# Output projection of a two-layer decoder trunk: order of its products, of its weight loads and of the block sums

## The chip, the cores and the metric

One core of a Trainium2 chip runs the whole program. The metric is the device time of one execution in microseconds (us), lower is better; the time before is the median of three executions, and the profile is of one further execution.

## The reference, cut to what matters

```python
for l in range(DEPTH):                      # DEPTH = 2, x is (1, 1024, 1024)
    h = rmsnorm(x, norm1[l])
    proj = h @ w_in[l]
    ...                                     # two attention branches o_a, o_b and two gates
    merged = g_a * (o_a @ w_br[l, :OUT_A]) + g_b * (o_b @ w_br[l, OUT_A:])
    x = x + merged @ w_o[l]                 # the output projection: the change is here
    h2 = rmsnorm(x, norm2[l])               # "norm" below
    up = h2 @ w_up[l]
    ...                                     # gated ConvFFN, down projection
return rmsnorm(x, norm_f)
```

## The kernel before, in words

Everything is kept transposed: a chunk of 128 features lies on the 128 partitions, and 512 tokens (half `n`, 0 or 1) lie along a row. A fp32 number is split in two parts, `hi` (a cast by ScalarE, line 129) and `lo` (a subtraction by VectorE, line 130), and one product of a 128-wide block is three matmuls: hi by hi, lo by hi, hi by lo (lines 891 to 893). Half of a contraction of 1024 takes four such blocks, so 12 matmuls; that is called **a product** here.

Ahead of the projection, a loop over 16 chunks (`todo`) multiplies the branch results with the gates (line 1451, tile `gin`), adds them to `mrg` (line 1456), and writes the merged chunk as `hh` (ScalarE, line 1415) and `hl` (GpSimd, line 1416). These are todo 0 to 15; the last four are chunk 6 and 7 of half 0 and chunk 6 and 7 of half 1. The four buffers `p4` that hold `gin` are used again by the tiles `wo_c` of `w_o`: the load of the first `wo_c` starts when todo 12 has been added, the second after todo 13, the third after 14, the fourth after 15.

The projection has 8 output chunks. Chunks 6 and 7 are done plainly, two products for each half (`chunk(n, e)`). Chunks 0 to 5 go in pairs (0,1), (2,3), (4,5) by a seven-product scheme (`p1` to `p7` for a pair). Its weights are sums of four blocks of a pair, made in place by GpSimd (`weight_sums`, lines 1146 to 1149), and its inputs are sums of blocks of the merged input: first `m_sum` (made earlier), second (lines 1265 and 1266, VectorE, in place), third `h_sum` (lines 1271 to 1273, GpSimd), fourth (lines 1278 and 1279, VectorE, in place). Each is split into `t_hi` and `t_lo` (the lists `S[1]` to `S[4]`) when it is made.

`items` lists the products in TensorE's order, and it is the list that sets the order around the change. Product `i` of the list is numbered from 0. Before:

0, 1 `chunk(0,6)`; 2, 3 `chunk(0,7)`; 4, 5 `chunk(1,6)`; 6 `p1(0)`; 7 `p3(0)`; 8 `p1(1)`; 9 `p3(1)`; 10 `p2(0)`; 11 `p2(1)`; 12 `p5(0)`; 13 `p6(0)`; 14 `p5(1)`; 15 `p6(1)`; 16 `p1(2)`; 17 `p7(0)`; 18 `p3(2)`; 19 `p7(1)`; 20 `p6(2)`; 21 `p5(2)`; 22 `p7(2)`; then, beside the norm of half 0, 23 `p2(2)`; 24 to 26 `p4`; 27, 28 `chunk(1,7)`.

Before product `i` is issued, `run` fetches raw weights up to product `i + 4`, splits weights up to product `i + 2` (`prepare`; for a `p1` the weights' sums of its pair follow at once), and makes the block sums that `merged_sums` plans for `i`. TensorE runs in exactly this order; the other engines' streams are set by a scheduler from the order of the code, and each engine then runs its stream in order.

When half 0 of `x` is complete, `norm(0)` sums its squares over features with small matmuls by `ones` (`nrm_t`, line 467), takes the root (ScalarE) and the reciprocal (VectorE, line 470), spreads the result with another group (`nrm_b`, line 476) and scales `x`. The squares are added up chunk by chunk in `norm_add` (line 420), on VectorE where `e % 3` is 1 and on GpSimd otherwise. `drive` interleaves it with products 23 to 28; `norm(1)` follows, interleaved with the first products of the ConvFFN (`u_ps`).

Of the kernel before, what the change touches and what calls it, by code (L numbers as in the profile page):

```python
# [6 lines left out]
F32 = mybir.dt.float32  # L7
# [8 lines left out]
P = 128  # L16
# [36 lines left out]
def trunk_kernel(ctx, tc, x, norm1, w_in, b_gate, w_br, w_o, norm2, w_up, conv_w, conv_b, w_down, norm_f, out, depth=None, probe=None):  # L53
# [355 lines left out]
    def norm_add(n, e, first=False, sub=slice(0, HF), adds=None):  # L409

        if first:
            if n == 0 or ACC[0] is None:
                both = sb.tile([P, 2, HF], F32, tag="ql", bufs=2, name="nrm")
                ACC[0], ACC[1] = both[:, 0, :], both[:, 1, :]
        acc = ACC[n]
        acc = acc[:, sub]
        sq = acc if first else small("sq")[:, sub]
        act.activation(sq, xc(n, e, sub), AF.Square)  # L418
        if not first:
            (adds or (dve if e % 3 == 1 else pool)).tensor_tensor(acc, acc, sq, ALU.add)  # L420
# [704 lines left out]
    def output_products(l, sums):  # L1125
# [4 lines left out]
        def columns(c):  # L1130
            return w_o[l][:, c * P : (c + 1) * P].rearrange("(k p) n -> p k n", p=P)

        def load_pairs():
            for p in range(3):
                if p < 2:
                    t = [sb.tile([P, 2, HF], F32, tag="p4", bufs=4, name="wo_c") for _ in range(2)]
                else:
                    both = sb.tile([P, 4, HF], F32, tag="ql", bufs=2, name="wo_p")
                    t = [both[:, 0:2, :], both[:, 2:4, :]]
                for c in range(2):  # L1140
                    nc.sync.dma_start(t[c].rearrange("p a (k n) -> p (a k) n", n=P), columns(2 * p + c))
                tiles[p] = [t[c][:, k, :] for c in range(2) for k in range(2)]

        def weight_sums(p):
            a11, a12, a21, a22 = tiles[p]
# [5 lines left out]
        def add(n, e, o, full=False):  # L1151
            dve.tensor_tensor(xc(n, e), xc(n, e), o, ALU.add)
            if full:
                norm_add(n, e, e == 6)

        def free(name):
            return lambda key: bank("ps", name)
# [13 lines left out]
        def chunk(n, e):  # L1171
            for k in range(2):
                items.append(
                    (("raw", e, k), (lambda key: plain.setdefault(key, bank("ps", "o_ps"))) , (n, e), lambda n=n, k=k: half(n, k), k == 0, k == 1,
                     (lambda o, n=n, e=e: add(n, e, o, True)) if k else None)
                )
# [36 lines left out]
        chunk(1, 7)  # L1213

        loaded, ready = {}, {}

# [17 lines left out]
                at[name] += 1  # L1234

        def start():
            load_pairs()
            until("fetch", fetch, 2)
            until("prepare", prepare, 2)

# [10 lines left out]
                    done(o)  # L1251
                yield

        return start, lambda: run(0, count), lambda: run(count, len(items))

    def merged_sums(keep):

        def split_into(t, i, r):
            if t not in S:
                new_s(t)  # L1260
            split(*S[t][i], r)

        def second(i):
            r, (h, lo) = keep[i], half(0, 1)[i]
            dve.tensor_tensor(r, f32(h), r, ALU.subtract)
            dve.tensor_tensor(r, r, f32(lo), ALU.add)
            split_into(2, i, r)

        def third(i):
            r, (ah, al), (bh, bl) = small("h_sum"), half(0, 1)[i], half(0, 0)[i]  # L1270
            pool.tensor_tensor(r, f32(al), f32(bl), ALU.subtract)
            pool.tensor_tensor(r, r, f32(ah), ALU.add)
            pool.tensor_tensor(r, r, f32(bh), ALU.subtract)
# [36 lines left out]
    def mixer(l, pending):  # L1310
# [71 lines left out]
        def gate_in(i):  # L1382
            if i < len(todo):
                n, e = todo[i]
                gt = gts[i] = sb.tile([P, 2, HF], F32, tag="p4", bufs=4, name="gin")
                nc.sync.dma_start(gt, gs[e, n])
                for ab in range(2):
                    act.activation(gt[:, ab, :], gt[:, ab, :], AF.Sigmoid, bias=bg[:, 0, ab * KD + e : ab * KD + e + 1])
# [9 lines left out]
                wbs.append(parts_)  # L1398

        kept, sums = {}, {}  # L1400

        def merged(n, e, m):
            if e < 4:
# [28 lines left out]
        for i, ab in order:  # L1432
            n, e = todo[i]
            sl = slice(n * HF, (n + 1) * HF)
            if i not in seen:
                if e == 0:
                    new_h(n)
                if i % 4 == 0:
                    wb = wbs.pop(0)
                if l and i in X_AT:  # L1440
                    x_in(X_AT.index(i) // 2, X_AT.index(i) % 2)
            gt = gts[i]
            ec = slice((e % 2) * P, (e % 2 + 1) * P)
            if "ab"[ab] not in oh:
                in_two("a")
            o = bank("st"[ab], "br_ps")
            (wh, wl), (xh, xl) = wb[ab], oh["ab"[ab]]
            for _ in product(o, [((wh[:, c, ec], wl[:, c, ec]), (xh[:, c, sl], xl[:, c, sl])) for c in range(2)]):
                pass
            with tc.high_priority(offset=AHEAD):  # L1450
                dve.tensor_tensor(gt[:, ab, :], gt[:, ab, :], o, ALU.mult)
# [4 lines left out]
            dve.tensor_tensor(m, gt[:, 0, :], gt[:, 1, :], ALU.add)  # L1456
# [598 lines left out]
```

## Time and profile before

| | before |
|---|---|
| median of three executions | 2776.66 us (2774.24 to 2783.27) |
| profiled execution, whole | 2783.72 us |
| its span, first to last instruction | 2781.9 us |
| TensorE busy | 2675.2 us, 96% |
| VectorE busy | 2182.6 us, 78% |
| ScalarE busy | 1343.6 us, 48% |
| GpSimd busy | 829.5 us, 30% |
| mean granted TensorE clock | 0.983 |

Times are from the start of the span. The projection of layer 0 begins at 632.1 us, that of layer 1 at 2005.9 us. A busy share is an average over stages with different limits, so it says little of a stage of 85 us; the stage is read from what TensorE waits for in it.

### The profile page before, as it was taken

Reading aid. Unit: us, or ns where it says so; the run is one execution under the profiler, and the core shown is the slowest. Engines: PE = TensorE matmul, PEld = TensorE weight load, DVE = VectorE, ACT = ScalarE, POOL = GpSimd, SP = SyncE. Lnnn points to the kernel's source line nnn. Section 1 sums busy time; section 2 is a strip of 40 time slices with the busy share of each in tenths; the row PEclk is TensorE's granted clock in tenths of the full one; section 3 lists DMA queues with packets and bytes.
Section 4 is the critical chain, followed back from the end, with each engine's and each line's share of the span. In section 5 each row is a group of like instructions: output and inputs, shape, how many; then the busy total and the mean of one; then the engine's idle time right before and its main releaser. Section 6 shows DMA issues by size and latency. Waiting matters only on the chain. (4 is left out here: it accounts for less than half of the span.)

```text
span 2781.9 us, 36907 instructions
## 1 busy us (share of the span) xinstructions
PE 2675.2 (96%) x13026; PEld 2232.8 (80%) x13026; DVE 2182.6 (78%) x3186; ACT 1343.6 (48%) x2484; POOL 829.5 (30%) x593
## 2 busy tenths in 40 slices
PE   8999999998899999999999999999988999999999
PEld 7877888886678888888888778888766788888888
DVE  5878866787689888897657887766977888988965
ACT  5666544463455555432345665434634555554225
POOL 2004133236224443321220042332451334443210
PEclk9999999999999999999999999999989999999999
DMA  4023499762134444688401235988602344346863
GB/s 149 27 84 111 130 244 233 206 238 68 53 111 147 152 152 144 217 324 317 151 33 46 80 118 152 254 211 232 223 19 57 121 160 166 137 154 239 322 260 122
DMA packets 391109, 442.56 MB, mean 159 GB/s; under 512 B 21276, under 2 KB 312460, under 8 KB 389388
## 3 DMA queue, kind: packets, MB, share of 16 engines
q1 hardware_dynamic: 390924, 440.20, 49.6%
q8 instruction: 103, 1.69, 0.3%
q14 instruction: 82, 0.67, 0.1%
HBM read 297.46 MB, written 142.67 MB: 158 GB/s over the span
## 5 line engine op out<-in xcount | busy, mean ns | idle before, releaser
L130 DVE TENSOR_TENSOR w_lo<-up_a,w_hi 128x512 fp32r<-128x512 f32 x240 | 237.0, 994 | 22.0 <-ACT w_hi L129 22.0
L129 ACT CAST w_hi<-up_a 128x512 fp32r<-128x512 f32 x240 | 149.3, 622 | 186.3 <-PE u_a L892 45.8
L1811 DVE TENSOR_TENSOR x<-x,d_ps 128x512 f32<-128x512 f32 (+1 forms) x228 | 152.6, 673 | 77.6 <-PE d_ps L1805 76.6
L1542 POOL TENSOR_TENSOR cv<-cv 128x512 f32<-128x512 f32 x88 | 131.8, 1509 | 248.6 <-DVE cv L1537 138.6
L129 ACT CAST w_hi<-in_a 128x512 fp32r<-128x512 f32 x140 | 86.8, 620 | 149.2 <-PE i_a L892 86.8
L130 DVE TENSOR_TENSOR g<-cv,g 128x512 fp32r<-128x512 f32 x154 | 152.3, 990 | 5.3 <-ACT g L129 2.8
L1803 PE MATMUL d_ps<-gd_in,w_hi 128*128 128x512 f32 (+1 forms) x340 | 130.2, 383 | 1.4 <-ACT w_hi L129 1.1
L1805 PE MATMUL d_ps<-gd_in,w_lo 128*128 128x512 f32 (+1 forms) x340 | 129.8, 382 | 0.0
L1804 PE MATMUL d_ps<-gd_in,w_hi 128*128 128x512 f32 (+1 forms) x340 | 129.7, 382 | 0.0
L130 DVE TENSOR_TENSOR w_lo<-w_raw,w_hi 128x512 fp32r<-128x512 f32 x140 | 105.5, 759 | 30.9 <-ACT w_hi L129 30.5
L891 PE MATMUL u_a<-hh,w_hi 128*128 128x512 f32 x320 | 124.7, 390 | 2.2 <-DVE u L1693 2.1
L891 PE MATMUL u_a<-t_hi,w_hi 128*128 128x512 f32 x320 | 124.6, 389 | 0.0
L892 PE MATMUL u_a<-t_lo,w_hi 128*128 128x512 f32 x320 | 124.5, 389 | 0.0
L893 PE MATMUL u_a<-hh,w_lo 128*128 128x512 f32 x320 | 124.5, 389 | 0.0
L892 PE MATMUL u_a<-hl,w_hi 128*128 128x512 f32 x320 | 124.5, 389 | 0.0
L893 PE MATMUL u_a<-t_hi,w_lo 128*128 128x512 f32 x320 | 124.5, 389 | 0.0
L1020 POOL TENSOR_TENSOR in_a<-in_a 128x512 f32<-128x512 f32 x28 | 38.0, 1357 | 277.5 <-DVE w_lo L130 277.5
L130 DVE TENSOR_TENSOR w_lo<-in_a,w_hi 128x512 fp32r<-128x512 f32 x140 | 114.3, 816 | 4.9 <-ACT w_hi L129 4.6
L420 POOL TENSOR_TENSOR nrm<-nrm,sq 128x512 f32<-128x512 f32 x29 | 40.8, 1406 | 255.8 <-ACT sq L418 255.1
L129 ACT CAST w_hi<-w_raw 128x512 fp32r<-128x512 f32 x140 | 86.4, 620 | 60.7 <-PE r_ps L156 15.8
L629 DVE TENSOR_TENSOR_SCAN stay<-stay,zero 128x128 f32<-128x128 f32 (+3 forms) x64 | 89.0, 1390 | 32.2 <-ACT stay L627 31.6
L1803 PE MATMUL d_ps<-gd_in,wd 128*128 128x512 f32 (+1 forms) x292 | 113.9, 390 | 0.0
(438 smaller groups left out, 9057.6 us busy)
## 6 DMA issues: line engine op xcount, KB each, us to landing
gd<-g SPq DMA_DIRECT2D x154, 512.0 KB, 3.5
gd_in<-gd SPq DMA_DIRECT2D x154, 512.0 KB, 6.3
up_a<-in_w_up_dram SPq DMA_DIRECT2D x80, 512.0 KB, 4.7
in_a<-in_w_in_dram SPq DMA_DIRECT2D x56, 512.0 KB, 5.7
w_raw<-in_w_in_dram SPq DMA_DIRECT2D x104, 256.0 KB, 2.9
t_kq<-tk SPq DMA_DIRECT2D x64, 384.0 KB, 8.5
wd_raw<-in_w_down_dram SPq DMA_DIRECT2D x22, 1024.0 KB, 11.9
gin<-gs SPq DMA_DIRECT2D x32, 512.0 KB, 4.0
```

The costliest lines, as they stand in the source:

```text
L129: act.copy(hi, src)
L130: dve.tensor_tensor(lo, src, f32(hi), ALU.subtract)
L420: (adds or (dve if e % 3 == 1 else pool)).tensor_tensor(acc, acc, sq, ALU.add)
L629: dve.tensor_tensor_scan(rev, rev, zero[:, 0:1].to_broadcast([P, L]), 1.0, ALU.mult, ALU.add)
L891: pe.matmul(o, w[0][:, c], rh, start=(first and i == 0), stop=False, skip_group_check=True)
L892: pe.matmul(o, w[0][:, c], rl, start=False, stop=False, skip_group_check=True)
L893: pe.matmul(o, w[1][:, c], rh, start=False, stop=(last and i == 3), skip_group_check=True)
L1542: return lambda: pool.tensor_tensor(dst, a, b, ALU.subtract)
L1803: pe.matmul(o[:, sub], wh[:, c], gh[:, sub], start=(i == 0 and k in (0, 4, 5)), stop=False, skip_group_check=True)
L1804: pe.matmul(o[:, sub], wh[:, c], gl[:, sub], start=False, stop=False, skip_group_check=True)
L1805: pe.matmul(o[:, sub], wl[:, c], gh[:, sub], start=False, stop=(i == m - 1), skip_group_check=True)
L1811: dve.tensor_tensor(x, x, o[:, sub], ALU.add)
```

## The change

In `items`, `p1(0)` and `p1(1)` move from places 6 and 8 to places 2 and 3, and `chunk(1,7)` moves ahead of the three `p4`. The list is then: 0, 1 `chunk(0,6)`; 2 `p1(0)`; 3 `p1(1)`; 4, 5 `chunk(0,7)`; 6, 7 `chunk(1,6)`; 8, 9 `p3(0)`, `p3(1)`; 10 to 23 as before; 24, 25 `chunk(1,7)`; 26 to 28 `p4`. The loads of the pairs' weights are issued one by one inside the loop over todo (from todo 12), and the first fetches and splits (`start`) are called there too. The plan of `merged_sums` is renumbered and calls `split_into(2, ...)` on its own. `drive` runs four steps of the products ahead of `norm(0)`. The square of half 0's chunk 5 is added by VectorE.

```diff
-        def load_pairs():
-            for p in range(3):
...
+        def load(i):
+            p, c = i // 2, i % 2
+            if p < 2:
+                t = sb.tile([P, 2, HF], F32, tag="p4", bufs=4, name="wo_c")
...
+            nc.sync.dma_start(t.rearrange("p a (k n) -> p (a k) n", n=P), columns(i))
...
             if full:
-                norm_add(n, e, e == 6)
+                norm_add(n, e, e == 6, adds=dve if (n, e) == (0, 5) else None)
...
         chunk(0, 6)
+        p1(0)
+        p1(1)
         chunk(0, 7)
         chunk(1, 6)
-        for f, p in ((p1, 0), (p3, 0), (p1, 1), (p3, 1), (p2, 0), (p2, 1)):
+        for f, p in ((p3, 0), (p3, 1), (p2, 0), (p2, 1)):
             f(p)
...
-        for f, p in ((p2, 2), (p4, 0), (p4, 1), (p4, 2)):
-            f(p)
+        p2(2)
         chunk(1, 7)
+        for p in range(3):
+            p4(p)
...
+    def merged_sums(keep):
...
+        def second(i):
+            r, (h, lo) = keep[i], half(0, 1)[i]
+            pool.tensor_tensor(r, f32(h), r, ALU.subtract)
+            pool.tensor_tensor(r, r, f32(lo), ALU.add)
...
     def merged_sums(keep):
...
         for i in range(4):
-            task(i // 2, lambda i=i: split_into(1, i, keep[i]))
-            task(2 + i, second, i)
-            task(6 + 2 * i, third, i)
-            task(8 + 2 * i, lambda i=i: split_into(3, i, third_r[i]))
+            task(1 + i // 2, lambda i=i: split_into(1, i, keep[i]))
+            task(4 + i, second, i)
+            task(8 + i, lambda i=i: split_into(2, i, keep[i]))
+            task(9 + i, third, i)
+            task(12 + i, lambda i=i: split_into(3, i, third_r[i]))
             task(16 + i, fourth, i)
-            task(22, lambda i=i: split_into(4, i, keep[i]))
+            task(24 + i // 2, lambda i=i: split_into(4, i, keep[i]))
...
             gate_in(i + 3)
+            if i == 12:
+                start()
+            if i >= 12:
+                load(i - 12)
...
-        start, early, rest = output_products(l, merged_sums(sums))
-        start()
+        load(4)
+        load(5)
         for _ in early():
             pass
...
-        drive(first_half(), rest(), 0.7)
+        drive(first_half(), rest(), 0.7, 4)
```

The file also defines the functions from `zeros` to `output_products` twice, with the same text, and `merged_sums` twice, with different text. In Python the later definition is the one that is called. The first `merged_sums`, the one with `second` on `pool`, is the earlier; the later one is the old function with the new plan, and in it `second` still reads:

```python
        def second(i):
            r, (h, lo) = keep[i], half(0, 1)[i]
            dve.tensor_tensor(r, f32(h), r, ALU.subtract)
            dve.tensor_tensor(r, r, f32(lo), ALU.add)
            split_into(2, i, r)
```

Lines after the change are about 330 larger for this reason (line 1451 is 1779, 1456 is 1784, 1415 is 1743, 1152 is 1476).

Three places of the new order, all in layer 1. First VectorE at the end of the loop over todo, before; `gin_18279` is todo 14 and `gin_18303` is todo 15, and `t_lo_18405` is a split of a first sum:

```order
L1451 TENSOR_TENSOR gin_18279<-gin_18279,br_ps_18327 128x512
L1451 TENSOR_TENSOR gin_18279<-gin_18279,br_ps_18335 128x512
L1456 TENSOR_TENSOR mrg_18343<-gin_18279 128x512
L1451 TENSOR_TENSOR gin_18303<-gin_18303,br_ps_18347 128x512
L130 TENSOR_TENSOR t_lo_18405<-m_sum_18058,t_hi_18404 128x512 x2
L1451 TENSOR_TENSOR gin_18303<-gin_18303,br_ps_18355 128x512
L130 TENSOR_TENSOR t_lo_18405<-m_sum_18168,t_hi_18404 128x512
L1456 TENSOR_TENSOR mrg_18363<-gin_18303 128x512
```

VectorE at the same place after; `gin_18287` is todo 14, `gin_18311` is todo 15, and `wo_c_18327` is the first loaded tile, with the weights of `p1(0)`:

```order
L1779 TENSOR_TENSOR gin_18287<-gin_18287,br_ps_18351 128x512
L130 TENSOR_TENSOR w_lo_18405<-wo_c_18327,w_hi_18404 128x512
L1779 TENSOR_TENSOR gin_18287<-gin_18287,br_ps_18359 128x512
L130 TENSOR_TENSOR t_lo_18436<-m_sum_18066,t_hi_18435 128x512
L1779 TENSOR_TENSOR gin_18311<-gin_18311,br_ps_18373 128x512
L1784 TENSOR_TENSOR mrg_18367<-gin_18287 128x512
L1779 TENSOR_TENSOR gin_18311<-gin_18311,br_ps_18381 128x512
L130 TENSOR_TENSOR t_lo_18436<-m_sum_18066,t_hi_18435 128x512
L1784 TENSOR_TENSOR mrg_18389<-gin_18311 128x512
```

The split of `p1(0)`'s weights now stands between the two gate products of todo 14, and a split of a first sum has come ahead of `mrg` of todo 14.

Second, ScalarE about products 6 to 9 before; `t_hi_18597` is the third sum's split, and the weights of `p3(0)`, `p1(1)` and `p3(1)` are `w_hi_18522`, `w_hi_18547` and `w_hi_18575`:

```order
L129 CAST w_hi_18522<-wo_c_18371 128x512
L418 ACTIVATE sq_18494<-x0_18091 128x512
L129 CAST w_hi_18547<-wo_c_18375 128x512
L129 CAST t_hi_18597<-h_sum_18555 128x512
L129 CAST t_hi_18455<-m_sum_18194 128x512
L129 CAST t_hi_18597<-h_sum_18601 128x512
L129 CAST w_hi_18575<-wo_c_18375 128x512
```

ScalarE there after; `t_hi_18699` is the third sum's split, `t_hi_18507` is the second sum's, and the weights of `p3(0)`, `p3(1)`, `p2(0)` and `p2(1)` are `w_hi_18551`, `w_hi_18574`, `w_hi_18597` and `w_hi_18617`:

```order
L129 CAST t_hi_18507<-m_sum_18066 128x512
L129 CAST t_hi_18507<-m_sum_18176 128x512
L129 CAST w_hi_18551<-wo_c_18327 128x512
L129 CAST t_hi_18507<-m_sum_18176 128x512
L129 CAST w_hi_18574<-wo_c_18371 128x512
L129 CAST t_hi_18507<-m_sum_18202 128x512
L418 ACTIVATE sq_18546<-x0_18099 128x512
L129 CAST t_hi_18507<-m_sum_18202 128x512
L129 CAST w_hi_18597<-w_raw_18549 128x512
L129 CAST t_hi_18699<-h_sum_18621 128x512
L129 CAST t_hi_18699<-h_sum_18645 128x512
L129 CAST w_hi_18617<-w_raw_18572 128x512
```

The first two casts of the third sum now stand ahead of the weights of product 11 instead of product 9, and each part of the second sum is cast twice (eight casts and eight subtractions where there were four of each).

Third, TensorE at the norm of half 0, before (`o_18948` is product 23) and after (`o_ps` is `chunk(1,7)`, products 24 and 25):

```order
L891 MATMUL o_a<-t_hi,w_hi 128x512
L892 MATMUL o_a<-t_lo,w_hi 128x512
L893 MATMUL o_a<-t_hi,w_lo 128x512
L467 MATMUL nrm_t<-ones,nrm 128x1 x4
L891 MATMUL o_18948<-hh_17965,w_hi 128x512
L892 MATMUL o_18948<-hl_17966,w_hi 128x512
```

TensorE after:

```order
L891 MATMUL o_ps<-hh_17973,w_hi 128x512
L892 MATMUL o_ps<-hl_17974,w_hi 128x512
L893 MATMUL o_ps<-hh_17973,w_lo 128x512
L467 MATMUL nrm_t<-ones,nrm 128x1 x4
L891 MATMUL o_ps<-hh_17973,w_hi 128x512
L892 MATMUL o_ps<-hl_17974,w_hi 128x512
```

`nrm_t` stands 24 matmuls later, behind products 23 and 24, and `nrm_b` is still 12 matmuls behind it; the `nrm_t` of half 1 keeps its place.

More of the change, by code (lines that the diff above doesn't have):

```diff
@@ L1131, in columns @@
             return w_o[l][:, c * P : (c + 1) * P].rearrange("(k p) n -> p k n", p=P)
-        def load_pairs():
-            for p in range(3):
[L1135 to L1142, printed above, removed]
+        def load(i):
+            p, c = i // 2, i % 2
+            if p < 2:
+                t = sb.tile([P, 2, HF], F32, tag="p4", bufs=4, name="wo_c")
+            else:
+                if c == 0:
+                    tiles["two"] = sb.tile([P, 4, HF], F32, tag="ql", bufs=2, name="wo_p")
+                t = tiles["two"][:, 2 * c : 2 * c + 2, :]
+            nc.sync.dma_start(t.rearrange("p a (k n) -> p (a k) n", n=P), columns(i))
+            tiles[p] = tiles.get(p, []) + [t[:, k, :] for k in range(2)]
         def weight_sums(p):
@@ L1236, in start @@
         def start():
-            load_pairs()
             until("fetch", fetch, 2)
@@ new lines, in pair_kq, with put @@
+    def pair_kq(dense, l, g, pr):
+        off = 256 * g + P * pr
+        def put(c, n, x, psum):
+            hi = small("kq_h", F32R)
+            lo = small("kq_l", F32R) if psum else x.bitcast(F32R)
+            hv, lv, xv = (t if t is x and psum else t.rearrange("p (r j) -> p r j", r=4) for t in (hi, lo, x))
+            if c:
+                act.mul(hv, xv, -SCALE)
+                dve.scalar_tensor_tensor(lv, xv, -SCALE, f32(hv), ALU.mult, ALU.subtract)
+            else:
+                act.copy(hv, xv)
+                dve.tensor_tensor(lv, xv, f32(hv), ALU.subtract)
+            for src, kind in ((hv, 2), (lv, 1)) if c else ((hv, 3), (lv, 4)):
+                there = tk[pr][:, :, 6 * (g - 1) + kind, n * P : (n + 1) * P]
+                nc.sync.dma_start(there.rearrange("r p j -> p r j"), f32(src))
+            if (c, n) == (1, 1):
+                dense.done.add(f"{g}{pr}")
+        return pair(dense, l, (OFF_KA + off, OFF_QA + off), True, put)
@@ L1400, in mixer @@
         kept, sums = {}, {}
+        start, load, early, rest = output_products(l, merged_sums(sums))
         def merged(n, e, m):
```

243 lines of the change are left out of this document (242 added, 1 removed).

## The prediction

> **What bounds the kernel now.** I read the page's head first, for the size of the thing, and then the table of windows over the places where the change works. Its columns are window and length, busy time and instructions of TensorE, its weight loads, VectorE, ScalarE and GpSimd, then granted clock, DMA share and GB/s. The windows are products 0 to 11 of layer 1, the same of layer 0, products 12 to 22 of layer 1, and product 23 up to the end of the wait before the second `nrm_t`.
>
> ```profile
> span 2781.9 us, 36907 instructions
> ```
>
> ```profile
> 2005.90:2059.93 54.03, 40.20 (x145) 30.34 (x144) 45.20 (x51) 16.15 (x29) 33.89 (x23) 0.84 0.17 48
> 632.10:684.74 52.64, 39.27 (x147) 30.09 (x146) 42.20 (x48) 15.43 (x27) 33.63 (x22) 0.87 0.20 55
> 2059.93:2090.00 30.07, 30.07 (x133) 24.59 (x131) 20.24 (x31) 13.40 (x23) 12.84 (x9) 1.00 0.06 18
> 2090.00:2125.50 35.50, 24.99 (x102) 19.89 (x101) 27.09 (x38) 14.34 (x25) 10.35 (x7) 0.89 0.14 38
> ```
>
> The third row is the measure: eleven products in 30.07 us, 2.73 us each, TensorE busy throughout at clock 1.00. Twelve at that rate would be 32.8 us; the first row has 54.03, so 21.3 us are lost there, 13.8 of them in waiting (54.03 less 40.20) and the rest in matmuls at a lower clock, 0.84. The second row says that layer 0 is the same stage over again, with 52.64. In the first row VectorE is busy 45.20 of 54.03 us and GpSimd 33.89: it is these two that prepare sums and splits. What TensorE waited for between 2005 and 2136 us (sum, times, longest):
>
> ```profile
> PE o L891 <- ACT w_hi L129: 6.7, 1, 6.7
> PE nrm_t L467 <- DVE nrm L420: 5.2, 1, 5.2
> PE o L891 <- DVE x L1152: 3.4, 2, 1.8
> PE nrm_t L467 <- POOL nrm L420: 3.4, 1, 3.4
> PE o L893 <- DVE w_lo L130: 1.9, 1, 1.9
> ```
>
> The largest is for ScalarE's cast of weights, so I followed ScalarE and GpSimd back from it:
>
> ```profile
> 2035.23 0.62 ACT L129 CAST t_hi<-h_sum 128x512 fp32r<-128x512 f32 x1 [7.78 <-POOL h_sum L1273]
> 2042.71 0.62 ACT L129 CAST w_hi<-wo_c 128x512 fp32r<-128x512 f32 x1 [5.61 <-POOL wo_c L1148]
> ```
>
> ```profile
> 2021.75 1.62 POOL L1147 TENSOR_TENSOR wo_c<-wo_c 128x512 f32<-128x512 f32 x1 [3.09 <-DVE w_lo L130]
> ```
>
> ScalarE itself was free. Its queue stood 7.78 us behind a cast of a third sum, and then 5.61 us for the weights' sum of product 9; GpSimd had to make both, one after the other, and had itself stood 3.09 us for VectorE's split of weights that it overwrites. So the first half is bound by the chain VectorE and GpSimd, not by TensorE.
>
> **The change part by part: what is not there.** The new list, the loads and the norm's lead are real. The move of the second sums to GpSimd is not: the definition that is called leaves `second` on VectorE, and splits each part of the second sums twice. TensorE's matmuls are the same in number; only their order differs. The extra splits are four casts of 0.62 (row of 2035.23) on ScalarE, which has 38 us free of 54.03, at nothing as long as that room stays; and four subtractions on VectorE, at 0.60 to 1.68 each (rows below), 2.4 to 6.7 us a layer, counted in VectorE's walk.
>
> **What VectorE and GpSimd cost each other.** Three VectorE operations with two inputs in SBUF (the sum of two tiles) that had GpSimd working beside them, then GpSimd alone, then VectorE with GpSimd idle:
>
> ```profile
> 2028.91 1.75 DVE L420 TENSOR_TENSOR nrm<-nrm,sq 128x512 f32<-128x512 f32 x1
> 2030.59 1.76 DVE L1266 TENSOR_TENSOR m_sum<-m_sum,hl 128x512 f32<-128x512 f32 x1
> 2032.27 1.77 DVE L130 TENSOR_TENSOR w_lo<-wo_c,w_hi 128x512 fp32r<-128x512 f32 x1
> ```
>
> ```profile
> 2058.54 1.27 POOL L1271 TENSOR_TENSOR h_sum<-hl 128x512 f32<-128x512 f32 x1
> ```
>
> ```profile
> 2122.85 0.68 DVE L1152 TENSOR_TENSOR x<-x,o_ps 128x512 f32<-128x512 f32 x1
> 2123.45 1.28 DVE L130 TENSOR_TENSOR w_lo<-w_raw,w_hi 128x512 fp32r<-128x512 f32 x2
> ```
>
> From start to start a VectorE operation takes 0.60 us alone and 1.68 when one of GpSimd meets it, so a meeting costs VectorE 1.08 us. The Trainium skill ("SBUF — State Buffer", section "SBUF: two separate sides") calls the pair of ports that the two engines share an exclusive lock held for a whole instruction, which a VectorE operation with two inputs in SBUF needs as well. The trace agrees in kind: alone GpSimd took 1.27. By the lock alone a meeting would cost the full 1.27; with the 15 meetings found below that would be 2.9 us more in each layer, and the sum would come to about 2759.
>
> **Products 0 to 11.** The loads now start from todo 12 on, in SP's order. What sets their start and landing before:
>
> ```profile
> 2002.11 0.38 SPq L1141 DMA_DIRECT2D wo_c<-in_w_o_dram  x1
> ```
>
> ```profile
> 2009.27 1.29 POOL L1146 TENSOR_TENSOR wo_c<-wo_c 128x512 f32<-128x512 f32 x1 [1.34 <-DMA wo_c<-in_w_o_dram]
> ```
>
> ```profile
> 2000.76 1.32 DVE L1456 TENSOR_TENSOR mrg<-gin 128x512 f32<-128x512 f32 x1
> 2003.38 0.69 DVE L1456 TENSOR_TENSOR mrg<-gin 128x512 f32<-128x512 f32 x1
> 2005.37 0.80 DVE L1456 TENSOR_TENSOR mrg<-gin 128x512 f32<-128x512 f32 x1
> 2006.09 0.67 DVE L1451 TENSOR_TENSOR gin<-gin,br_ps 128x512 f32<-128x512 f32 x1
> 2011.03 1.77 DVE L1456 TENSOR_TENSOR mrg<-gin 128x512 f32<-128x512 f32 x1
> ```
>
> ```profile
> wo_c<-in_w_o_dram SPq DMA_DIRECT2D x8, 512.0 KB, 5.6
> wo_p<-in_w_o_dram SPq DMA_DIRECT2D x4, 512.0 KB, 8.1
> ```
>
> The first load is issued when todo 12 is added (2002.08), the second when todo 13 is (2004.07); GpSimd got the second one's data at 2009.27, 5.2 us later, and 5.2 is what I take for each, near the median of 5.6 in the row of issues; 8.1 is the upper end. The first then lands at 2007.3, is cast by 2007.9, and its subtraction is done at 2008.5. This subtraction now stands in VectorE's queue between the gate products of todo 14 and 15 (first order rows), so both wait behind a DMA. From 2006.09 to 2012.80 VectorE did six operations, 1.12 us each; the four up to the `mrg` of todo 14 end at 2013.0 instead of 2006.2. The third load, which that `mrg` releases and `p1(1)` needs, lands at 2018.2, its cast ends at 2018.8, and with the subtractions queued ahead its `lo` is there at about 2021.4. `p1(1)`, the fourth product, was due at 2005.9 plus 3 times 2.73, 2014.1, and has its hi-by-lo matmul some 0.5 us in: TensorE stands about 6.8 us there, a wait that before did not have, and `p1(1)` ends near 2025.4.
>
> What is late after that is VectorE. From 2008.5 until the `lo` of product 11 the order has 42 operations on it, 34 with two inputs in SBUF and 8 that read PSUM; 18 GpSimd operations stand in that stretch, of which some three fall outside it or beside PSUM reads. So 15 at 1.68 and 27 at 0.60, 41.4 us: 2049.9. As a check on this way of counting: the first window row has 51 operations in 45.20 us, 0.89 each, and this gives 0.99. With that `lo` only the last third of each matmul triple is late, so product 11 ends 2.4 us later, 2052.3. One spell of low clock comes on top; its price is that of product 11 before:
>
> ```profile
> 2055.52 0.47 PE L891 MATMUL o<-hh,w_hi 128*128 128x512 f32 x1 [1.84 <-DVE x L1152]
> 2056.58 0.63 PE L892 MATMUL o<-hl,w_hi 128*128 128x512 f32 x1
> ```
>
> It began after a wait of 1.84, its matmuls went from 0.47 to 0.63, and it ran from 2055.52 to 2059.93, 4.4 us, 1.7 over 2.73. So product 12 starts at 2054.0 and not 2059.93: **5.9 us** gained. The bounds: with both first loads at 8.1 the walk is up to 5.8 later, and nothing is left, 0.1; if VectorE keeps up, product 11 ends 8 times 2.73 behind `p1(1)`, at 2047.2, 12.7 gained. I take 5.9 since VectorE's share in the first row (45.20 of 54.03) says that it is nearly full. Why anything is gained at all: the third sums' casts stood ahead of product 9 on ScalarE and now stand ahead of product 11, so the 7.78 and the 5.61 no longer come in a row before one product.
>
> At nothing: the raw weights of products 6 and 7 now stand behind the loads in SP's queue and would land near 2025, three products before use (8.2 us if that cover is gone); the splits of the fourth sums, moved beside products 12 to 22, where VectorE is busy 20.24 of 30.07.
>
> **The norms.** Before, the chain behind product 22 was waited for, and so was that behind product 28:
>
> ```profile
> 2093.43 1.40 PE L467 MATMUL nrm_t<-ones,nrm 128*128 128x1 f32 x8 [3.41 <-POOL nrm L420]
> 2099.97 1.46 PE L476 MATMUL nrm_b<-ident,ss 128*128 128x128 f32 x8
> 2125.49 1.84 PE L467 MATMUL nrm_t<-ones,nrm 128*128 128x1 f32 x8 [5.25 <-DVE nrm L420]
> 2132.03 1.05 PE L476 MATMUL nrm_b<-ident,ss 128*128 128x128 f32 x8
> ```
>
> ```profile
> 2118.27 1.70 POOL L420 TENSOR_TENSOR nrm<-nrm,sq 128x512 f32<-128x512 f32 x1 [2.40 <-ACT sq L418]
> ```
>
> Product 23 starts at T = 2090.0. Now 24 matmuls, 5.45 us, stand ahead of `nrm_t`; the chain (x added, square 0.63, an addition on VectorE of 0.69) is done 2.8 us after T, so no wait. With 1.40, twelve matmuls (2.73) and 1.46, `nrm_b` ends at T + 11.0, before at T + 11.4, and 24 matmuls more are done by then. What comes after is the three `p4`: from the end of `nrm_b` (2101.43) to the end of GpSimd's addition for `p4(2)` (2119.97) it was 18.5 us before, less 1.04 for one meeting that goes, 17.5; this addition is now the last one. So the second `nrm_t` starts at T + 28.5, before T + 35.5. But nine VectorE operations of the ConvFFN that came ahead of it before (2117.55 to 2124.65 less the `x` addition, 6.5 us) now fall behind it, and stand ahead of the reciprocal and of the `u_ps` matmuls between: they start at T + 25.6, end at T + 32.1, and with 3.9 us for those matmuls `nrm_b` starts at T + 36.0, before T + 42.0. **6.0 us** gained; at least the 3.41 of the first wait, at most both, 8.7.
>
> **The sum.** Layer 0 has the same order and nearly the same window, so twice: 2 x (5.9 + 6.0) = 23.8 us. Against the profiled execution, 2783.7, that is 2759.9. It lies 7.06 us over the median of 2776.66, so the median should be **2753 us**. From the bounds of the middle alone the sum goes from 12.2 (2765) to 37.4 (2739).
>
> **The rivals.**
> *VectorE and GpSimd exclude each other all the way (slower).* If all 34 operations meet one of GpSimd, the walk from 2008.5 gives 2037.8 + 1.08 x 34 = 2074.5 for product 12, 14.6 later than before; less 6.0 at the norm that is 8.6 a layer, 2776.7 + 17.2 = 2794. It decides from 26 meetings on. For it: the extra subtractions, and the rows of 2028.91 to 2032.27, three meetings in a row. Against it: only 18 GpSimd operations stand there.
> *VectorE keeps up (more gained).* Middle 12.7, norms 8.7, 42.8 in all: 2734. Against it: VectorE's 45.20.
> *The waits only move (little).* The wait for the third load takes the place of the wait for the cast, middle 0, norms 3.4 a layer, 6.8 us: 2770. For it: the loads depend on the last todos, whose queue the change itself makes late.
> *The change doesn't do what it says* is sure for the second sums and is in the forecast by the extra splits.
>
> **How the numbers follow.** Forecast 0.62, more 0.10, little 0.13, slower 0.15. About 0.3%, 8.3 us, is what a measurement of this kernel can tell from no change. The forecast with its bounds and the case of more lie over it: faster 0.72; little is same, 0.13; slower 0.15. The range goes from 2739, the lower bound of the forecast, to 2772, the case of little and the 2.4 us by which the runs' lowest lies off their median; outside are the slow rival and half of the fast one.
>
> **What would show it.** Right: `nrm_t` of half 0 without a wait and a second wait of some 4 us; one wait of 5 to 8 us in product 3 for `w_lo`; product 12 about 48 us after product 0; no cast waiting for line 1148 ahead of product 9. Wrong: the stretch of products 0 to 11 still 54 us or longer, with VectorE's busy time up and its operations at 1.7 us each; or the loads landing over 8 us after their release.

## The result, and the profile after

The changed kernel takes 2767.28 us (median of five, 2763.22 to 2768.40) against 2776.66 (median of five, 2773.01 to 2783.27): the measured ratio is 0.9962, 95% interval 0.9945 to 0.9978 (the two medians alone would give 0.9966). By the medians it is 9.4 us faster. The forecast had 23.7 us; its range, 2739 to 2772, holds the result, near the end that the prediction gave to "the waits only move". The head of the page of the profiled execution, and the same four stretches as before (products 0 to 11 of layer 1 and of layer 0, products 12 to 22, and product 23 up to the second `nrm_t`):

```profile
span 2765.5 us, 36926 instructions
```

```profile
2000.42:2051.96 51.54, 37.64 (x146) 29.30 (x144) 50.57 (x57) 18.64 (x32) 30.84 (x19) 0.90 0.20 57
632.14:685.39 53.25, 39.96 (x145) 30.55 (x146) 52.52 (x57) 18.14 (x31) 32.05 (x21) 0.87 0.19 54
2051.96:2081.88 29.92, 29.92 (x134) 24.77 (x132) 22.91 (x34) 13.18 (x24) 18.37 (x12) 1.00 0.06 18
2081.88:2108.43 26.55, 21.08 (x101) 17.37 (x99) 22.77 (x33) 13.53 (x23) 9.22 (x6) 0.96 0.17 50
```

The last row is the gain: 26.55 us where there were 35.50 (of these 8.95 us, 2.0 go again between the second `nrm_t` and the second `nrm_b`: 6.55 us before, 8.54 after). The first two are the disappointment: 51.54 instead of 54.03 in layer 1, and 53.25 instead of 52.64 in layer 0. Their third busy time is VectorE's: 50.57 of 51.54, without a pause. The four largest of TensorE's waits in layer 1 (sum, times, longest):

```profile
PE o L891 <- DVE x L1476: 6.7, 2, 5.6
PE nrm_t L467 <- POOL nrm L420: 5.5, 1, 5.5
PE o_a L893 <- DVE w_lo L130: 4.3, 1, 4.3
PE o_a L891 <- ACT w_hi L129: 2.1, 1, 2.1
```

The wait of 6.7 for the cast and that of 3.4 for the first norm are gone. The 4.3 and the 2.1 are both at `p1(1)`, product 3, and are its forecast wait; the 5.6 at the top was not forecast. It is at product 8, `p3(0)`:

```profile
2038.29 0.76 PE L891 MATMUL o<-hh,w_hi 128*128 128x512 f32 x1 [5.60 <-DVE x L1476]
```

Line 1476 is `add`, the addition of a finished product to `x`. Results in PSUM that are tagged `ps` have two buffers; product 8 takes the one of `chunk(0,7)`, products 4 and 5. VectorE's rows around it:

```profile
2001.39 1.36 DVE L130 TENSOR_TENSOR w_lo<-wo_c,w_hi 128x512 fp32r<-128x512 f32 x1 [3.18 <-ACT w_hi L129]
...
2009.58 3.43 DVE L130 TENSOR_TENSOR t_lo<-m_sum,t_hi 128x512 fp32r<-128x512 f32 x2
2012.93 1.28 DVE L1591 TENSOR_TENSOR m_sum<-hh,m_sum 128x512 f32<-128x512 f32 x2
2014.14 1.74 DVE L130 TENSOR_TENSOR w_lo<-wo_c,w_hi 128x512 fp32r<-128x512 f32 x1
...
2028.30 0.67 DVE L1476 TENSOR_TENSOR x<-x,o_a 128x512 f32<-128x512 f32 x1
2028.90 1.18 DVE L130 TENSOR_TENSOR w_lo<-w_raw,w_hi 128x512 fp32r<-128x512 f32 x1
2030.00 1.77 DVE L1592 TENSOR_TENSOR m_sum<-m_sum,hl 128x512 f32<-128x512 f32 x1
2031.70 1.77 DVE L1591 TENSOR_TENSOR m_sum<-hh,m_sum 128x512 f32<-128x512 f32 x1
2033.39 2.35 DVE L130 TENSOR_TENSOR t_lo<-m_sum,t_hi 128x512 fp32r<-128x512 f32 x2
2035.66 0.68 DVE L130 TENSOR_TENSOR w_lo<-wo_c,w_hi 128x512 fp32r<-128x512 f32 x1
...
2037.47 0.68 DVE L1476 TENSOR_TENSOR x<-x,o_ps 128x512 f32<-128x512 f32 x1
...
2043.48 0.68 DVE L130 TENSOR_TENSOR w_lo<-w_raw,w_hi 128x512 fp32r<-128x512 f32 x1
...
2050.69 0.68 DVE L1476 TENSOR_TENSOR x<-x,o 128x512 f32<-128x512 f32 x1
```

The row of 2037.47 is the addition of `chunk(0,7)`. Ahead of it stand second sums and their splits, which are due at product 13. The row of 2043.48 is the split for product 11, at which the forecast's walk ended; the row of 2050.69 frees the buffer that product 12 takes. The row of 2014.14 is the subtraction that `p1(1)` waits for. Ahead of it stand two splits of first sums and two additions of second sums, due at products 12 and 13. ScalarE had made its cast by 2010.83, and that cast came right behind one that waited for the last `mrg`:

```profile
2009.69 0.62 ACT L1743 CAST hh<-mrg 128x512 fp32r<-128x512 f32 x1 [1.17 <-DVE mrg L1784]
2010.22 0.61 ACT L129 CAST w_hi<-wo_c 128x512 fp32r<-128x512 f32 x1
```

The DMA engines moved this third load from 2007.3 to 2009.5, so it was there before its cast began: both waits of product 3 end on VectorE's queue, not on the load.

### The profile page after: what moved, and what is told of

Its sections match the earlier page's. It is cut to its first block, busy times and chain, and to the rows that moved or that the text cites. A ratio compares the mean times of both kernels' runs of the same rounds, so it can differ in the third digit from the quotient of the medians.

```text
span 2765.5 us, 36926 instructions
## 1 busy us (share of the span) xinstructions
PE 2665.7 (96%) x13026; PEld 2226.5 (81%) x13026; DVE 2191.3 (79%) x3196; ACT 1346.6 (49%) x2492; POOL 830.5 (30%) x591
## 3 DMA queue, kind: packets, MB, share of 16 engines
q1 hardware_dynamic: 390924, 440.20, 49.8%
## 5 line engine op out<-in xcount | busy, mean ns | idle before, releaser
L129 ACT CAST w_hi<-up_a 128x512 fp32r<-128x512 f32 x240 | 149.4, 623 | 184.4 <-PE u_a L892 45.4
L129 ACT CAST g<-cv 128x512 fp32r<-128x512 f32 x154 | 94.9, 616 | 40.9 <-POOL cv L1874 29.7
```

Of the source, the lines that this page charges most:

```text
L129: act.copy(hi, src)
```

## The experiments

Ratios are to runs of the kernel before on the same chip; for the experiments there were three chips, with medians of before of 2777.19 to 2778.79, so small differences are to be read from the ratios and the traces. Where a wait just ahead of product 12 left a low clock in the second stretch, as with the other PSUM buffers, the two columns belong together. From the traces, the time from product 0 to product 12, and from product 12 to the second `nrm_b`, in us, layer 0 / layer 1:

| kernel | products 0 to 11 | 12 to second `nrm_b` | median | ratio to before (95%) |
|---|---|---|---|---|
| before | 52.6 / 54.0 | 71.9 / 72.1 | 2776.66 | |
| changed | 53.2 / 51.5 | 65.6 / 65.0 | 2767.28 | 0.9962 (0.9945 to 0.9978) |
| norms only | 52.8 / 54.0 | 65.1 / 65.1 | 2767.67 | 0.9966 (0.9954 to 0.9978) |
| first products only | 52.7 / 51.7 | 72.0 / 72.1 | 2776.35 | 0.9991 (0.9982 to 0.9999) |
| single split | 52.3 / 51.7 | 65.3 / 65.6 | 2766.81 | 0.9959 (0.9945 to 0.9973) |
| second sums on GpSimd | 60.1 / 62.0 | 65.6 / 65.6 | 2784.30 | 1.0019 (1.0010 to 1.0028) |
| `p1(1)` later | 56.1 / 54.8 | 65.6 / 65.6 | 2769.99 | 0.9974 (0.9964 to 0.9983) |
| other PSUM buffers | 52.2 / 51.2 | 67.2 / 67.3 | 2769.62 | 0.9971 (0.9960 to 0.9981) |
| no third sums | 46.4 / 45.7 | 65.6 / 65.6 | 2754.01 | 0.9914 (0.9899 to 0.9930) |
| single split, no fourth sums | 49.8 / 50.1 | 65.6 / 65.6 | 2759.93 | 0.9939 (0.9927 to 0.9952) |
| together | 50.0 / 50.6 | 64.1 / 67.5 | 2759.88 | 0.9937 (0.9923 to 0.9951) |
| buffers, single split | 49.7 / 49.5 | 64.6 / 64.6 | 2758.34 | 0.9931 (0.9919 to 0.9944) |
| and short third sums | 47.1 / 44.8 | 64.0 / 64.1 | 2750.42 | 0.9904 (0.9891 to 0.9918) |
| together, short third sums | 48.0 / 46.6 | 64.4 / 63.8 | 2753.36 | 0.9917 (0.9903 to 0.9930) |

### Which half of the change gained

Norms only, the last part of the change on the kernel before:

```diff
-        for f, p in ((p2, 2), (p4, 0), (p4, 1), (p4, 2)):
-            f(p)
+        p2(2)
         chunk(1, 7)
+        for p in range(3):
+            p4(p)
...
-        drive(first_half(), rest(), 0.7)
+        drive(first_half(), rest(), 0.7, 4)
```

together with the addition for chunk 5 and the fourth splits' places.

> The kernel before with the change's last part alone: chunk(1,7) ahead of the three p4, four steps of the products ahead of the norm, the addition of the square of chunk 5 on VectorE, the splits of the fourth sums at 24 and 25. If the gain of the change is all from the norms: product 23 to the second nrm_b takes 35 us instead of 42, in both layers, the whole falls by 12 to 14 us, to 2763 to 2765, at or under the changed kernel. If the first part brings a gain of its own as forecast (5.9 a layer): 2771 or more.

And the reverse, the changed kernel with that part put back:

> The changed kernel with that last part undone: only the moved first products, their loads and splits and the new plan of the sums are left. If the first part brings nothing: within 2 us of before, 2775 to 2779, its stretch of products 0 to 11 51 to 54 us in both layers, and layer 0's start 1 us later. By the forecast it would be 11.8 us under before, 2765.

Measured: 2767.67 and 2776.35. The norms alone give as much as the whole change (0.9966 beside 0.9962). In the traces the first products gain 2.3 us in layer 1 and nothing in layer 0; in time 0.9 parts in a thousand (0.1 to 1.8).

### Is it the number of VectorE's operations?

```diff
             dve.tensor_tensor(r, r, f32(lo), ALU.add)
-            split_into(2, i, r)
```

> The changed kernel with its second sums split once instead of twice: four casts and four subtractions fewer in each layer, nothing else. Theory V (products 0 to 11 are bound by VectorE's queue: it is busy 50.57 of 51.54 us there, and product 8 waits 5.60 us for an addition that stands behind sums and splits): the addition that frees product 8 comes 2.4 to 6.7 us sooner, the stretch falls from 51.5 to about 48 us in layer 1 and from 53.3 to about 50 in layer 0, the whole by 5 to 8 us, to 2759 to 2762. Theory L (the third load and its split, for which product 3 waits 4.3 to 4.8 us, set the stretch): no change, 2765 to 2768.

Measured 2766.81, a ratio of 0.9959 beside 0.9962: the gain that theory V promised did not come, and theory V falls in that form. Theory L, that the loads set the stretch, was not shown by that either, because the trace of this run has VectorE still busy 48.71 of 51.72 us, and the same wait:

```profile
1993.05:2044.77 51.72, 38.39 (x146) 29.67 (x144) 48.71 (x53) 16.51 (x29) 32.29 (x20) 0.87 0.19 55
```

```profile
PE o L891 <- DVE x L1476: 5.5, 1, 5.5
```

```profile
2029.63 0.68 DVE L1603 TENSOR_TENSOR m_sum<-hh,m_sum 128x512 f32<-128x512 f32 x1
2030.23 0.67 DVE L1476 TENSOR_TENSOR x<-x,o_ps 128x512 f32<-128x512 f32 x1
```

Line 1603 is a fourth sum, due at products 26 to 28, ahead of the addition that product 8 waits for: the scheduler had drawn later work, second sums and this fourth sum, into the places of the removed splits. Whether this refill ate the gain was tried by leaving the fourth sums' additions out of this version:

```diff
-            dve.tensor_tensor(r, f32(h), r, ALU.subtract)
-            dve.tensor_tensor(r, r, f32(lo), ALU.add)
+            pass
```

> The single-split version with the fourth sums' additions left out: eight additions of VectorE a layer are not done, their splits are made from the second sums. Theory A (VectorE is without a pause up to product 12; what is taken from it is filled with work that is due later, the fourth sums, so that only the work that stands ahead of product 8 and of product 12 in its queue counts): in the single-split version the fourth sums' additions took the places of the removed splits; without them the addition that frees product 8 comes 1 to 2 us sooner and none stands ahead of product 12, the stretch 49 to 50 us instead of 51.7 and 52.3, the whole 4 to 5 us under the single-split version, 2762. If VectorE's amount doesn't decide: 2766 to 2768 as there.

Measured 2759.93, 6.9 under the single-split version, with 49.8 and 50.1 in the stretch, as theory A has it. In the trace the addition for product 8 comes 0.8 us sooner after product 0 in layer 1, a little under the forecast 1 to 2. So in the single-split version the places that had come free were filled, and nothing was gained. This run does less work, so it shows that the fourth sums' additions cost time there, and no more; what the single split is worth with other buffers is in the last experiments.

### Is it the place in the queue?

`p1(1)` two places later:

```diff
         p1(0)
+        chunk(0, 7)
         p1(1)
-        chunk(0, 7)
         chunk(1, 6)
```

> The changed kernel with the second moved product, p1(1), two places later, behind chunk(0,7). Theory Q (what product 8 waits for is the place of two rows in VectorE's queue, the weights' subtraction of product 8 and the addition of chunk(0,7) that frees its PSUM buffer; before them stand sums and splits that are due only at products 13 to 17): the wait of p1(1) (4.3 to 4.8 us) goes, and the addition comes five operations sooner, so product 8 begins some 4 us sooner after product 0; the stretch 47 to 48 us instead of 51.5 in layer 1, 49 to 50 in layer 0, the whole 2759 to 2762. Rival A (the amount of VectorE's work up to product 12 decides, wherever it stands): 51 to 53 us as now, 2765 to 2768.

Measured 2769.99, a ratio of 0.9974 beside 0.9962, whose intervals overlap; in the traces the stretch is 2.9 and 3.3 us longer. In layer 1 the wait of `p1(1)` for its subtraction fell from 4.3 to 0.5, but `chunk(1,6)` then waited 4.8 for a subtraction and product 9 6.4 for the addition of `chunk(1,6)`: theory Q was wrong here, and by its stretch, 56.1 and 54.8, so was rival A. Moving a wait that stands ahead of a full VectorE does not take it away.

Other PSUM buffers for products 8 and 9:

```diff
-            items.append((("tile", p, 1), free("o_3"), p, b22, True, True, lambda o: add(0, 2 * p, o)))
+            items.append((("tile", p, 1), (lambda key: bank("s", "o_3")) if p < 2 else free("o_3"), p, b22, True, True, lambda o: add(0, 2 * p, o)))
```

> The changed kernel with the results of p3(0) and p3(1) (products 8 and 9) in other PSUM buffers, so that product 8 needs no addition of product 5. Theory Q: in layer 1 product 8 begins when its cast is there, at about its due time, and then stands for its subtraction, which VectorE ends 1.8 us before that addition; the 5.6 us become 3 to 4, the whole falls by 2 to 4 us, to 2763 to 2765. Rival B (the buffer is the whole of the wait): 5.6 in layer 1 and 1.9 in layer 0 go with the low clock behind them, 2757 to 2759. Rival A: nothing, the wait turns up at another product.

Measured 2769.62, no gain (0.9971 beside 0.9962), where theory Q had 2763 to 2765. Product 8's 5.6 fell to 2.7 for the subtraction, a little under Q's 3 to 4, and the rest came up at product 12, as rival A has it:

```profile
2050.77 0.47 PE L891 MATMUL o<-t_hi,w_hi 128*128 128x512 f32 x1 [4.39 <-DVE x L1476]
```

```profile
2049.93 0.69 DVE L1476 TENSOR_TENSOR x<-x,o 128x512 f32<-128x512 f32 x1
```

Product 12 needs the buffer of product 10, whose addition comes at 2049.93 because VectorE's queue has had no pause until then. There are two points in that queue, and the later one decides: freeing the first alone gains nothing. Behind the wait product 12 itself takes 4.4 us at a granted clock of 0.62, where 2.73 is usual, which is why this version's second stretch is 67.2 and 67.3 and not 65.6.

### Is it GpSimd?

The third sums left out; VectorE's order up to the weights of product 10 is the same:

```diff
-            pool.tensor_tensor(r, f32(al), f32(bl), ALU.subtract)
-            pool.tensor_tensor(r, r, f32(ah), ALU.add)
-            pool.tensor_tensor(r, r, f32(bh), ALU.subtract)
-            third_r[i] = r
+            third_r[i] = keep[i]
```

> The changed kernel without GpSimd's third sums: twelve additions of GpSimd a layer are left out, and the splits of the third sums are made from the second sums. VectorE's order from the last mrg to the weights of product 10 stays the same row for row. Theory Q with meetings at 1.08 us each: nine of the meetings ahead of the addition that frees product 8 are gone, it comes 9 to 10 us sooner, product 8 doesn't wait, the stretch falls to 44 to 46 us in layer 1 and 46 to 49 in layer 0, the whole by 10 to 14 us, to 2753 to 2757. If VectorE's operations are long there for another reason than GpSimd, or rival A holds by number of operations: nothing changes, 2765 to 2768.

Measured 2754.01, 13.3 under the changed kernel, by leaving out operations of an engine for which TensorE waited nowhere in that stretch:

```profile
1992.15:2037.88 45.73, 37.18 (x145) 29.48 (x144) 44.19 (x58) 19.90 (x35) 18.50 (x12) 0.89 0.22 64
```

```profile
2017.55 0.69 DVE L1592 TENSOR_TENSOR m_sum<-m_sum,hl 128x512 f32<-128x512 f32 x1
2018.15 0.69 DVE L1591 TENSOR_TENSOR m_sum<-hh,m_sum 128x512 f32<-128x512 f32 x1
```

58 operations where there were 57, in 44.19 us instead of 50.57. The same two second sums took 1.77 each at 2030.00 and 2031.70 in the changed kernel, and 0.69 here. The addition that frees product 8 comes 7.4 us sooner after product 0, seven meetings' worth and not the nine of the forecast. So the price of meeting GpSimd is real, and taking it away shortens the stretch by 5.8 and 6.9 us. VectorE is nearly full even so (44.19 of 45.73).

### What the change's words say

Second sums on GpSimd, split once:

```diff
-            dve.tensor_tensor(r, f32(h), r, ALU.subtract)
-            dve.tensor_tensor(r, r, f32(lo), ALU.add)
-            split_into(2, i, r)
+            pool.tensor_tensor(r, f32(h), r, ALU.subtract)
+            pool.tensor_tensor(r, r, f32(lo), ALU.add)
```

> The changed kernel with the second sums made by GpSimd and split once, as the change's words have it: VectorE loses 8 additions and 4 subtractions a layer, GpSimd gains 8 additions of 1.3 to 1.7 us. Theory V: VectorE loses 12 operations of 0.6 to 1.7 us, product 8 no longer waits, each stretch falls to 45 to 47 us, where the waits of product 2 and 3 and low clock are left; the whole by 11 to 14 us, to 2753 to 2756. Theory L: 2765 to 2768. A rival G (GpSimd's queue becomes the bound, since its weights' sums and third sums come later): the stretch stays at 51 or goes over it, with a wait of products 9 to 14 for sums by GpSimd.

Measured 2784.30, slower than before. In layer 1 ScalarE shows it: first a row for a second sum's cast that waits 6.95 us for GpSimd, and behind it in the queue the weights of `p1(1)`:

```profile
2026.27 0.62 ACT L129 CAST t_hi<-m_sum 128x512 fp32r<-128x512 f32 x1 [6.95 <-POOL m_sum L1592]
2026.80 0.61 ACT L129 CAST w_hi<-wo_c 128x512 fp32r<-128x512 f32 x1
```

```profile
2027.46 0.79 PE L891 MATMUL o_a<-hh,w_hi 128*128 128x512 f32 x1 [12.71 <-ACT w_hi L129]
```

It is rival G, though the wait is at product 3 and not at 9 to 14, with the pattern that the kernel before had at product 9: a cast that is not due, on an in-order queue, ahead of one that is. In layer 0 the largest wait is another: 8.2 us at product 8 for VectorE's addition, behind five additions of fourth sums and a split of some 1.7 us each. That the called definition left the second sums on VectorE was the faster of the two.

### Versions that keep all the work

The parts were put together in four versions: other buffers, single split and chunk 5's square on VectorE in both halves ("buffers, single split"); that with `p1(1)` later ("together"); and each of the two with the third sums made from the second, by two additions of GpSimd instead of three, which also can't start early:

```diff
-            r, (ah, al), (bh, bl) = small("h_sum"), half(0, 1)[i], half(0, 0)[i]
-            pool.tensor_tensor(r, f32(al), f32(bl), ALU.subtract)
-            pool.tensor_tensor(r, r, f32(ah), ALU.add)
-            pool.tensor_tensor(r, r, f32(bh), ALU.subtract)
+            r, (h, lo) = small("h_sum"), half(1, 0)[i]
+            pool.tensor_tensor(r, keep[i], f32(h), ALU.subtract)
+            pool.tensor_tensor(r, r, f32(lo), ALU.subtract)
```

> A version that keeps all the work: the changed kernel with p1(1) behind chunk(0,7), products 8 and 9 in other PSUM buffers, the second sums split once, and the last square of each half (chunk 5) added by VectorE. Theory Q: 5 us a layer from the first half, 1 us a layer from the second norm's wait (5.5 us for GpSimd's addition of 1.7): 2754 to 2758. Rival A: only the last, 2764 to 2766.

> All the work is kept: the changed kernel with the second sums split once, products 8 and 9 in other PSUM buffers, and chunk 5's square added by VectorE in both halves. Theory A: product 8 waits 2 to 3 us for its subtraction only, product 12 for the addition of product 10, which has two to four operations fewer ahead; the stretch 49 to 50 us, 1 us a layer from the second norm: 2760 to 2763. If the two waits of the single-split and the other-banks version just return: 2766.

> The same with the third sums made from the second: two additions of GpSimd for each instead of three, and not before the second sum is there. All the work is kept. Meetings at 1.08 us each (the run without third sums): four GpSimd operations fewer, and five or six fewer ahead of product 8's subtraction: the stretch 46 to 47 us, the whole 2753 to 2757. Rival: the third sums come so late that ScalarE's casts of them hold up the weights of products 10 to 12, as before the change (7.78 and 5.61 us of waiting): the stretch 50 or more, 2762 or more.

> The version with everything together (p1(1) behind chunk(0,7), other PSUM buffers, single split, chunk 5's square on VectorE) and the third sums made from the second by two additions of GpSimd. All the work is kept. By meetings at 1.08 us: 3 to 4 us a layer under that version's 50.0 and 50.6, the whole 2752 to 2756. By the rival of late third sums: 2760 or more.

Measured 2759.88, 2758.34, 2750.42 and 2753.36. The first missed its 2754 to 2758, which rested on theory Q; the second and third came out some 2 us under theirs, the fourth within. That `p1(1)` later does harm here too is seen in layer 1's trace alone (50.6 and 67.5 against 49.5 and 64.6); the times of the first two are not apart. With the other buffers the single split does gain: 49.7 and 49.5 against 52.2 and 51.2, though the same fourth sums are drawn in, since four subtractions fewer stand ahead of the addition that frees product 12. The third is the fastest of all, 0.9904 (0.9891 to 0.9918) of before, and no late third sum held TensorE up. Layer 1's stretch and its two largest waits:

```profile
1987.66:2032.41 44.75, 36.04 (x145) 27.82 (x144) 43.49 (x49) 15.75 (x29) 27.50 (x17) 0.92 0.23 67
```

```profile
PE o_a L893 <- DVE w_lo L130: 4.3, 1, 4.3
PE o_a L891 <- ACT w_hi L129: 2.2, 1, 2.2
```

Product 8's waits are down to 0.8 us and product 12's to 0.2; the two that are left stand at product 3, and in layer 0 `chunk(1,6)` still waits some 4 in all. VectorE is still busy 43.49 of 44.75.

## Why the prediction was right and wrong

**The norms: right.** Forecast 6.0 us a layer; the table has 6.4 and 7.1. `nrm_t` of half 0 has no wait. GpSimd's last addition ended at T + 26.5 and not T + 28.5 (T = 2081.88), so the second `nrm_t` came 2 us sooner than forecast, and it waited 5.5 us, not 4, since TensorE was there sooner still. From there on the steps agree: the operations ahead of the reciprocal ended at T + 31.8 (forecast 32.1), `nrm_b` began at T + 35.1 (36.0):

```profile
2106.86 1.52 POOL L420 TENSOR_TENSOR nrm<-nrm,sq 128x512 f32<-128x512 f32 x1 [1.96 <-ACT sq L418]
```

```profile
2113.55 0.17 DVE L470 RECIPROCAL ss<-ss 128x4 f32<-128x4 f32 x1
```

```profile
2116.97 1.05 PE L476 MATMUL nrm_b<-ident,ss 128*128 128x128 f32 x8
```

Some 0.5 us a layer is given back between the second `nrm_b` and the first `u_a` product of the ConvFFN (40.4 us before, 40.8 after).

**The price of a meeting and the walk: right, up to where it was read.** From the end of the first split (2002.75) to the end of product 11's split (2044.16) VectorE took 41.4 us for 42 operations; the forecast had 41.4, and 15 meetings is the number that fits it. The rows of 2030.00 and 2031.70 begin 1.70 apart, 1.10 more than the 0.60 of an operation alone, so the price per meeting stands by itself. With 1.27 for each of the 15, an estimate from the lock that the Trainium skill describes ("SBUF — State Buffer", section "SBUF: two separate sides"), the walk would be 44.3; the measurement decides for about 1.1.

At `p1(1)` the forecast had one wait of 6.8; measured were 2.1 and 4.3, 6.5 together, and its `lo` was there 15.5 us after product 0, as forecast. That agreement is luck: the load was there 9.1 us after product 0, not 12.3, and VectorE's queue held its cast and its subtraction up by as much.

**The failed step: "With that `lo` only the last third of each matmul triple is late, so product 11 ends 2.4 us later".** The walk was read off at one point, the split of product 11, and the only way in which VectorE could hold TensorE in it was through weights. It also holds it through PSUM. The addition of `chunk(0,7)`, ten operations earlier in the same walk, ended at 2038.15, and product 8 began at 2038.29. From there on TensorE needs four products, 10.9, one more wait of 1.06 and the 1.7 of a low clock: 2051.96. The forecast's way from the split (2044.16 and 2.4 and 1.7) ends at 2048.3, 3.7 us too soon. Even without product 8's wait, the addition of product 10 ends at 2051.37, 7.2 us behind the split at which the walk stopped, since fourth sums stand between; this is what the run with other buffers shows. The walk led on to it gives 2049.9 + 7.2 = 2057.1 against 2059.93, 2.8 us gained instead of 5.9; measured were 2.5 in layer 1.

**"Layer 0 has the same order and nearly the same window, so twice": wrong.** Its stretch got 0.6 longer where 5.9 was forecast. Before, it was 1.4 shorter than layer 1's, so there was less to gain. VectorE's order is not the same either: from the first split to product 11's it has 44 operations and not 42, and product 11's split ends 45.4 us after product 0, 1.4 later than the walk had it (in layer 1 it was 43.7, forecast 44.0). The rest is the failed step again: product 8 begins when the addition of `chunk(0,7)` ends, 39.5 after product 0, and product 12 comes 13.7 behind that as in layer 1, 3.7 later than the way through the weights. 5.9 less 1.4, 1.4 and 3.7 is the -0.6.

**The sum.** Norms 13.5 for a forecast of 12; first products 1.9 for a forecast of 11.8; less 0.9 given back and 1.9 by which layer 0's product 0 came later after the start of the loop over todo in this trace (53.6 us, before 51.7; the other versions of it have 51.4 to 53.6, so it is not shown to be of the change). In the two traces all stages that the change touches, from the loop over todo to the ConvFFN, take 12.7 us less; the other 3.7 of the 16.4 between the spans lie in stages with the same instructions: from `u_a` of layer 1 to the end, for one, before took 609.6 us, and the thirteen other profiles 607.2 to 608.1, the changed kernel 607.7. They are not of the change. The medians' 9.4 lies with 12.7 inside the interval (6.1 to 15.3 us). That the profiled execution of before lay 7 us over its median was taken off the forecast, rightly.

**The rivals.** That the waits only move (0.13) was the truth of the first half: its gain is near 0. But it had the wait at the third load alone, and norms of 3.4; that wait came, the one at the PSUM buffers came on top, and the norms gained 6.4 to 7.1. The slower case did not come: 15 meetings fit the walk, not 26.

What stays open: what the two waits of product 3 would be if its weights' cast and subtraction stood ahead of the splits and sums that are due later. No run tried that.

## What to carry to other kernels

Where an in-order engine is full, walk its queue to every instruction that another engine waits for, and take the largest of "ready there plus what is left to do"; the additions that free PSUM buffers count as much as the weights. Work taken from such an engine can gain nothing if the scheduler fills its place with work that is due later, so look at the new order before pricing a removal. And an engine that nobody waits for can still cost time, by stretching the operations of its neighbour.

## What the runs showed of the hardware that was not expected

VectorE's additions from PSUM kept their 0.67 us in the middle of GpSimd's stretch (row of 2028.30), where those with both inputs in SBUF took 1.77. Stages with the same instructions differ from execution to execution: from the start to the loop over todo of layer 0 the profiled runs took 577.4 to 581.4 us, more than the whole effect of the first half of the change, while the stretch from product 12 to the second `nrm_b` came out within 0.6 us (65.0 to 65.6) in all runs with the changed norms as they are in this change, but for the run with other buffers, where a wait ahead of product 12 left a low clock in it.
